# Encoder layer on one core: the down-projection with tokens on partitions in all its columns, and paired one-column products

## The chip, the core and the metric

The kernel runs on one core of a Trainium2 chip. The engines named here are TensorE (PE; its weight loads are listed as PEld), VectorE (DVE), ScalarE (ACT) and the queue of SyncE (SP) that issues most transfers. The metric is the time of one execution on the device in microseconds (us); several runs give a median. The profile is that of one execution, with starts counted from its first instruction.

## The reference

One encoder layer over 256 tokens of width 2048, in float32. What matters here is its end:

```python
x = x + concatenate([y_a, y_b, y_c]) @ w_out[i]        # 2048 x 2048
h = rmsnorm(x, norm_ffn[i])
up = dwconv3(h @ ffn_w_up[i], ...)                     # 2048 -> 2 x 5632
gate, val = jnp.split(up, 2, axis=-1)
x = x + (jax.nn.silu(gate) * val) @ ffn_w_down[i]      # 5632 -> 2048
return rmsnorm(x, norm_final)
```

`rmsnorm` divides a token's 2048 values by the root of their mean square and multiplies them by a weight for each channel.

## The kernel before

**Products.** Every weight arrives from memory as a float32 chunk `raw` of 128x1024 (512 KB; four buffers), is rounded by ACT to `hi` and its remainder taken by DVE as `lo = raw - hi` (three buffers each); this is `load_split` (lines 100 to 117: the cast is L115, the subtraction L116). Activations are kept as such pairs too (`actA`, `actB`, `yT`, `gT`), so that a product takes three terms: hi by hi, lo by hi and hi by lo.

**Channels on partitions.** In the input, output and up-projections, and in most of the down-projection, a weight block of 128x128 stands still in PE and the activations move (`chunk_products`, L144 to L152): for each block of 128 input channels one product with 512 columns (L151: the activation's hi and lo parts of 256 tokens side by side) and one with 256 columns (L152: the weight's lo part by the activation's hi part). Below, such a pair is called one step. `proj_tile` makes one tile of 128 output channels so: 16 steps in the up-projection, 44 in the down-projection. ACT then copies the second half of the sums (L159), and DVE adds the two.

**The down-projection.** Output tiles 0 to 11 (`MD` = 12 of 16) are made that way, by 12 x 44 = 528 steps; to each DVE adds the residual `xT`, ACT squares it (L647) and DVE adds the squares into `acc3`. The last 512 channels have the tokens on partitions: the activation `gT` stands still (128 tokens, hi or lo) and 512 columns of weights move. `products` (L775 to L783) gives three products of 512 columns for each half `h` of the tokens and each block `k`. There the residual enters the sums by eight products with the identity (L759). The first four chunks of those weights are loaded early into `kept`; the half `h = 0` uses them first, and `h = 1` at the very end. `sum_cols(acc3)` (L176, two one-column products) gives the squares of the first 12 tiles. `finish(h)` (L729 to L753) squares the 512 columns, makes the factor of each token, spreads it over partitions by a product (L746), scales everything and sends it out in five transfers for each half: one with tokens on partitions, four with channels on partitions.

**Order.** The tile framework sets the order on each engine from the program order, priorities (a load has an offset of `AHEAD` = 150) and buffers. Each engine executes its own queue in order. `settle` (L132) puts one product of one moving column into the PE's stream and pins its place; it is called twice at the start of the output projection (L659, L660) and once in the up-projection after tile 2 (L693). The one-column product is in float32 and shows as two records, and so does every other product of plain float32 that is not a transposition.

## Time and profile before

| | us |
|---|---|
| median of 3 runs (1071.21 to 1071.91) | 1071.64 |
| the profiled execution | 1071.91 |
| its span, first to last instruction | 1070.0 |
| PE busy | 1059.6 |
| DVE busy | 788.9 |
| ACT busy | 578.6 |

The profiled execution is 1.9 us longer than its span, and it is the longest of the three, 0.27 us above the median. PE is busy nearly all the time. Its products overlap in the records (each row's duration is longer than the distance to the next start), so the distance between starts tells what a product costs in the stream.

### The profile page before, as it was taken

How to read it: one execution, taken by the hardware profiler on the slowest of the kernel's cores; microseconds unless marked ns; L12 is line 12 of the kernel's file. 1: busy time of each engine (PE TensorE's matmuls, PEld its weight loads, DVE VectorE, ACT ScalarE, POOL GpSimd, SP SyncE). 2: the span in 40 equal slices, each digit the busy share in tenths (PEclk: the TensorE clock that was granted, in tenths of full speed). 3: DMA queues.
4: the chain of work that ended last, by engine and by line, in shares of the span. 5: the costliest groups of instructions: out<-in, count | busy, mean ns of one | idle time of the engine just before them, and what ended most of it. 6: DMA issues, size and time to landing. Idle time of an engine off the chain costs nothing.

```text
span 1070.0 us, 15760 instructions
## 1 busy us (share of the span) xinstructions
PE 1059.6 (99%) x5974; PEld 923.6 (86%) x5974; DVE 788.9 (74%) x1241; ACT 578.6 (54%) x876; POOL 1.3 (0%) x14
## 2 busy tenths in 40 slices
PE   9999999999999999999999999999999999999997
PEld 9888898888888888888888888888888888888885
DVE  7899998987768778787777777787876454565344
ACT  7766555555556555555555555555555444454332
POOL 0000000000000000000000000000000000000000
PEclk9999999999999999999999999999999999999999
DMA  8776555655666555655566555655565655666452
GB/s 290 244 229 210 161 164 171 232 172 185 196 194 182 186 186 188 182 192 181 193 181 192 181 192 182 190 184 185 189 188 178 190 183 182 225 214 199 142 191 78
DMA packets 61875, 202.83 MB, mean 190 GB/s; under 512 B 6919, under 2 KB 11752, under 8 KB 61672
## 3 DMA queue, kind: packets, MB, share of 16 engines
q1 hardware_dynamic: 61512, 201.45, 59.2%
q8 instruction: 46, 0.75, 0.3%
q10 hardware_dynamic: 288, 0.39, 0.1%
q14 instruction: 29, 0.24, 0.1%
HBM read 199.72 MB, written 2.10 MB: 189 GB/s over the span
## 4 chain that ended last, share of the span: by engine, by line
PE 96%; DVE 1%; DMA 1%; ACT 1%; issue 0%; SPq 0%; DVEq 0%; ACTq 0%
PE mm L151 57%; PE mm L152 29%; PE mm L781 2%; PE mm L783 2%; PE mm L782 2%; PE mm L264 1%; PE mm L263 1%; PE mm L265 1%; DVE lo L116 1%; DMA head<-in_w_v 1%; PE aux L141 0%; PE aux L142 0%; DMA raw<-in_w_in 0%; PE aux L489 0%; PE aux L140 0%
## 5 line engine op out<-in xcount | busy, mean ns | idle before, releaser
L115 ACT CAST hi<-raw 128x1024 fp32r<-128x1024 f32 (+1 forms) x362 | 373.4, 1031 | 443.7 <-PE mm L151 222.8
L116 DVE TENSOR_TENSOR lo<-raw,hi 128x1024 fp32r<-128x1024 f32 (+1 forms) x362 | 434.6, 1201 | 239.6 <-ACT hi L115 239.0
L151 PE MATMUL mm<-actB,hi 128*128 128x512 f32 x1408 | 497.9, 399 | 0.0
L152 PE MATMUL mm<-actB,lo 128*128 128x256 f32 x1408 | 395.3, 281 | 0.0
L151 PEld LDWEIGHTS mm<-actB,hi 128*128 128x128 f32 x1408 | 264.5, 188 | 66.0 <-DVE actB L668 0.3
L152 PEld LDWEIGHTS mm<-actB,lo 128*128 128x128 f32 x1408 | 265.9, 189 | 0.0
L151 PE MATMUL mm<-gT,hi 128*128 128x512 f32 x528 | 186.6, 399 | 0.0
L152 PE MATMUL mm<-gT,lo 128*128 128x256 f32 x528 | 148.3, 281 | 0.0
L151 PE MATMUL mm<-actA,hi 128*128 128x512 f32 x416 | 148.0, 398 | 0.0
L151 PEld LDWEIGHTS mm<-gT,hi 128*128 128x128 f32 x528 | 99.2, 188 | 24.8
L152 PE MATMUL mm<-actA,lo 128*128 128x256 f32 x416 | 116.2, 279 | 0.0
L152 PEld LDWEIGHTS mm<-gT,lo 128*128 128x128 f32 x528 | 99.7, 189 | 0.0
L151 PEld LDWEIGHTS mm<-actA,hi 128*128 128x128 f32 x416 | 78.1, 188 | 16.9
L151 PE MATMUL mm<-yT,hi 128*128 128x512 f32 x256 | 89.3, 395 | 0.0
L152 PEld LDWEIGHTS mm<-actA,lo 128*128 128x128 f32 x416 | 78.5, 189 | 0.1
L152 PE MATMUL mm<-yT,lo 128*128 128x256 f32 x256 | 71.0, 278 | 0.0
L408 ACT ACTIVATE o<-ev,par 128x256 f32<-128x256 f32 x106 | 63.4, 598 | 7.2 <-DVE ev L403 5.7
L151 PEld LDWEIGHTS mm<-yT,hi 128*128 128x128 f32 x256 | 48.0, 188 | 11.1
L410 DVE SCALAR_TENSOR_TENSOR o<-ev,par,o 128x255 f32<-128x255 f32 x106 | 51.2, 483 | 3.3
L159 ACT COPY sb<-mm 128x256 f32<-128x256 f32 x142 | 51.8, 365 | 0.0
L409 DVE SCALAR_TENSOR_TENSOR o<-ev,par,o 128x255 f32<-128x255 f32 x106 | 50.7, 478 | 0.4 <-ACT o L408 0.4
L152 PEld LDWEIGHTS mm<-yT,lo 128*128 128x128 f32 x256 | 48.1, 188 | 0.0
(226 smaller groups left out, 819.2 us busy)
## 6 DMA issues: line engine op xcount, KB each, us to landing
raw<-in_w_up SPq DMA_DIRECT2D x176, 512.0 KB, 3.5
raw<-in_w_down SPq DMA_DIRECT2D x60, 512.0 KB, 3.6
raw<-in_w_in SPq DMA_DIRECT2D x56, 512.0 KB, 3.6
raw<-in_w_out SPq DMA_DIRECT2D x32, 512.0 KB, 3.5
raw<-in_w_last SPq DMA_DIRECT2D x22, 512.0 KB, 3.5
raw<-in_w_v SPq DMA_DIRECT2D x8, 384.0 KB, 4.4
raw<-in_w_down SPq DMA_DIRECT2D x12, 256.0 KB, 2.6
head<-in_w_v SPq DMA_DIRECT2D x7, 384.0 KB, 6.2
```

The costliest lines, as they stand in the source:

```text
L115: nc.scalar.copy(hi[:, s], raw[:, s])
L116: nc.vector.tensor_sub(lo[:, s], raw[:, s], hi[:, s].bitcast(F32))
L151: nc.tensor.matmul(ps, hi[:, s], act[:, k, :, :], start=k == 0, stop=False)
L152: nc.tensor.matmul(ps[:, :L], lo[:, s], act[:, k, 0, :], start=False, stop=k == nk - 1)
L159: nc.scalar.copy(sb, ps[:, L:])
L263: nc.tensor.matmul(o, actA[:, k, 0, t], hi[:, s], start=k == 0, stop=False)
L408: nc.scalar.activation(o, s, AF.Identity, bias=col(b), scale=col(w1))
L409: nc.vector.scalar_tensor_tensor(o[:, 1:], s[:, :L - 1], col(w0), o[:, 1:], op0=ALU.mult, op1=ALU.add)
L410: nc.vector.scalar_tensor_tensor(o[:, :L - 1], s[:, 1:], col(w2), o[:, :L - 1], op0=ALU.mult, op1=ALU.add)
L781: nc.tensor.matmul(acc[h], lh, hi[:, s], start=False, stop=False)
L782: nc.tensor.matmul(acc[h], lh, lo[:, s], start=False, stop=False)
L783: nc.tensor.matmul(acc[h], ll, hi[:, s], start=False, stop=False)
```

## The change

All 2048 output channels of the down-projection now have the tokens on partitions, as four groups of 512 channels (`NG` = 4). For each group, `group(g)` puts the residual into two accumulators (one for each half of the tokens) by eight transpositions on PE (`is_transpose=True`, where there were eight products with the identity for the last group alone). Then 22 chunks follow, each with `products` for both halves. At a group's end `squares_tok` (ACT, its output in a `raw` buffer) sums the squares of 512 columns, and `weigh` (DVE) multiplies by the final norm's weight `gtok` into the place of `xT`; `gtok` is now 128x2048. The last group still begins and ends with the kept chunks. `finish` has no product any more; it scales four pieces of 128x512 and sends each out. `acc3`, its one-column sums, the products of `finish` and the split of the last chunk into halves of 256 columns are gone.

`settle` now makes two one-column products at a time; the second call in the output projection is removed. Two pads in the memory of the core are 64 bytes smaller.

```diff
@@ -34,7 +34,6 @@
-MD = KT - NL // P
@@ -130,7 +129,9 @@
     def settle():
-        tc.keep_in_program_order(nc.tensor.matmul(aux()[:, 0:1], ones, ones[:, 0:1], start=True, stop=True))
+        pc = aux()
+        for h in range(2):
+            tc.keep_in_program_order(nc.tensor.matmul(pc[:, h:h + 1], ones, ones[:, 0:1], start=True, stop=True))
     def split(hi, lo, src):
         nc.scalar.copy(hi, src)
@@ -242,7 +243,7 @@
     def v_product(then):
         pv = [[psm.tile([P, 512], F32, tag="mm", name="mm") for _ in range(2)] for _ in range(2)]
-        p1.tile([P, 56], F32, name="pad_y")
+        p1.tile([P, 40], F32, name="pad_y")
         head = p1.tile([P, KT // 2, D_GM], F32, tag="yT", name="head")
         for k in range(KT):
             if k == 0:
@@ -657,7 +658,6 @@
             chunk_products(head[m], w_out(m), yT, c, KT)
             if c == m == 0:
                 settle()
-    settle()
     for m in range(KT):
         ps, sb = (head[m], second_half(head[m])) if m < 2 else proj_tile(w_out(m), yT, KT)
         x = xT[:, m, :]
@@ -672,7 +672,7 @@
     p2 = ctx.enter_context(tc.tile_pool(name="p2", bufs=1))
-    p2.tile([P, 64], F32, name="pad_g")
+    p2.tile([P, 48], F32, name="pad_g")
     gT = p2.tile([P, NFF, 2, L], F32R, name="gT")
     rbc2 = p2.tile([P, L], F32, name="rbc_ffn")
@@ -701,98 +701,96 @@
         split(gT[:, j, 0, :], gT[:, j, 1, :], sg)
-    acc3 = p2.tile([P, L], F32, name="acc3")
-    gtok = p2.tile([P, NL], F32, name="gtok")
+    gtok = p2.tile([P, D], F32, name="gtok")
     nc.sync.dma_start(gtok, a["gfin"].partition_broadcast(P))
     NKC = CW // NL
     NC = NFF // NKC
+    NG = D // NL
     NKEEP = KT * L // CW
     kept = big.tile([P, NKEEP, 2, CW], F32R, tag="actA", name="kept")
-    chunks = {}
-    for m in range(MD):
-        c = m - (MD - 1 - NKEEP)
-        if 0 <= c < NKEEP:
-            chunks[c] = load_split(a["w_last"][c], CW, into=(kept[:, c, 0, :], kept[:, c, 1, :]))
-        ps, sb = proj_tile(lambda c, n: a["w_down"][m, c][:, :n], gT, NFF)
-        x = xT[:, m, :]
-        nc.vector.tensor_add(sb, x, sb)
-        nc.vector.tensor_add(x, ps[:, :L], sb)
-        sumsq(acc3, x, m)
-        nc.scalar.activation(x, x, AF.Copy, scale=col(C_GFIN + m))
+    ssq = p2.tile([P, 2, NG], F32, name="ssq")
     rest = p2.tile([P, 2], F32, name="rest")
     c15 = p2.tile([P, 1], F32, name="c15")
     nc.vector.memset(c15, 1.5)
-    def finish(h, ps):
...
-    def products(h, c):
-        hi, lo = chunks[c]
+    res = xT.rearrange("p (g k) l -> p g (k l)", g=NG)
+    def group(g):
+        acc = [bank() for _ in range(2)]
+        for h in range(2):
+            for i in range(NL // P):
+                nc.tensor.matmul(acc[h][:, i * P:(i + 1) * P], xT[:, g * NL // P + i, h * P:(h + 1) * P], ident,
+                                 is_transpose=True, start=i == 0, stop=False)
+        return acc
+    def products(acc, h, w, c, last):
+        hi, lo = w
         for i in range(NKC):
             k = NKC * c + i
             s = slice(i * NL, (i + 1) * NL)
             lh, ll = (gT[:, k, j, h * P:(h + 1) * P] for j in range(2))
             nc.tensor.matmul(acc[h], lh, hi[:, s], start=False, stop=False)
             nc.tensor.matmul(acc[h], lh, lo[:, s], start=False, stop=False)
-            nc.tensor.matmul(acc[h], ll, hi[:, s], start=False, stop=False)
+            nc.tensor.matmul(acc[h], ll, hi[:, s], start=False, stop=last and i == NKC - 1)
+    def squares_tok(g, h, ps):
+        sq = wp.tile([P, CW], F32, tag="raw", name="raw", bufs=4)
+        nc.scalar.activation(sq[:, :NL], ps, AF.Square, accum_out=ssq[:, h, g:g + 1])
+    def out(g, h):
+        return res[:, g, h * NL:(h + 1) * NL]
+    def weigh(g, h, ps):
+        nc.vector.tensor_mul(out(g, h), ps, gtok[:, g * NL:(g + 1) * NL])
+    chunks = {}
+    for g in range(NG - 1):
+        acc = group(g)
+        for c in range(NC):
+            if g == NG - 2 and c % 4 == 3 and c // 4 < NKEEP:
+                j = c // 4
+                chunks[j] = load_split(a["w_down"][NG - 1, j], CW, into=(kept[:, j, 0, :], kept[:, j, 1, :]))
+            w = load_split(a["w_down"][g, c], CW)
+            for h in range(2):
+                products(acc, h, w, c, c == NC - 1)
+        for h in range(2):
+            squares_tok(g, h, acc[h])
+            weigh(g, h, acc[h])
+    nc.vector.tensor_add(rest, ssq[:, :, 0], ssq[:, :, 1])
+    nc.vector.tensor_add(rest, rest, ssq[:, :, 2])
+    nc.vector.tensor_scalar(rest, rest, 1.0 / D, EPS_RMS, op0=ALU.mult, op1=ALU.add)
+    def finish(h, ps):
+        g = NG - 1
+        squares_tok(g, h, ps)
+        weigh(g, h, ps)
+        v, s_, y, w, r = (tmp(f"fin{i}", 1) for i in range(5))
+        nc.scalar.activation(s_, ssq[:, h, g:], AF.Sqrt, scale=1.0 / D, bias=rest[:, h:h + 1])
+        nc.vector.tensor_scalar(v, ssq[:, h, g:], 1.0 / D, rest[:, h:h + 1], op0=ALU.mult, op1=ALU.add)
+        nc.vector.reciprocal(y, s_)
+        nc.vector.scalar_tensor_tensor(w, y, -0.5, y, op0=ALU.mult, op1=ALU.mult)
+        nc.vector.scalar_tensor_tensor(w, w, v, c15, op0=ALU.mult, op1=ALU.add)
+        nc.vector.tensor_mul(r, w, y)
+        for g in range(NG):
+            o = out(g, h)
+            if g == 1:
+                nc.scalar.activation(o, o, AF.Copy, scale=r)
+            else:
+                nc.vector.tensor_scalar(o, o, r, None, op0=ALU.mult)
+            (nc.scalar if g == 1 else nc.sync).dma_start(a["out"][h, :, g * NL:(g + 1) * NL], o)
+    acc = group(NG - 1)
     for c in range(NC):
         if c >= NKEEP:
-            chunks[c] = load_split(a["w_last"][c], CW)
-        (last_products if c == NC - 1 else products)(0, c)
+            chunks[c] = load_split(a["w_down"][NG - 1, c], CW)
+        products(acc, 0, chunks[c], c, c == NC - 1)
         if c >= NKEEP:
-            products(1, c)
-        if c == NKEEP:
-            pc = sum_cols(acc3)
-            nc.vector.tensor_scalar(rest, pc[:, 0:2], 1.0 / D, EPS_RMS, op0=ALU.mult, op1=ALU.add)
+            products(acc, 1, chunks[c], c, False)
     for c in range(NKEEP):
-        (last_products if c == NKEEP - 1 else products)(1, c)
+        products(acc, 1, chunks[c], c, c == NKEEP - 1)
         if c == 1:
             finish(0, acc[0])
     finish(1, acc[1])
```

**PE in the output and up-projections.** `L133` before is `L134` after, the one-column products of `settle`; around it stand the pairs of a step. Before, in three places:

```order
L151 MATMUL mm<-yT,hi 128x512
L152 MATMUL mm<-yT,lo 128x256
L133 MATMUL aux<-ones 128x1
L151 MATMUL mm<-yT,hi 128x512
...
L152 MATMUL mm<-actB,lo 128x256
L176 MATMUL aux<-ones,acc_2522 128x1 x2
L151 MATMUL mm<-actB,hi 128x512
...
L152 MATMUL mm<-actB,lo 128x256
L133 MATMUL aux<-ones 128x1
L151 MATMUL mm<-actB,hi 128x512
```

The first of these places comes twice, 24 steps apart. After the change, the one place in the output projection and the one in the up-projection:

```order
L152 MATMUL mm<-yT,hi 128x512
L153 MATMUL mm<-yT,lo 128x256
L134 MATMUL aux<-ones 128x1 x2
L152 MATMUL mm<-yT,hi 128x512
...
L153 MATMUL mm<-actB,lo 128x256
L134 MATMUL aux<-ones 128x1 x2
L152 MATMUL mm<-actB,hi 128x512
```

The second one-column product of the pair stands directly behind the first; the place 24 steps on holds none.

**PE at the end of group 1, after the change.** `mm_8810` is group 1's accumulator of the second half, `mm_9652` and `mm_9653` are group 3's, `mm_9221` and `mm_9222` group 2's (whose transpositions were already made at the end of group 0); L735 is the last term of a block, L723 a transposition, L733 and L734 the first two terms; names in brackets are what an instruction waits for:

```order
L735 MATMUL mm_8810<-hi_9198,gT_3393 128x512
L723 MATMUL mm_9652<-ident_80,xT_2519 128x128 [waits DVE_49,PE_49]
L723 MATMUL mm_9652<-ident_80,xT_2519 128x128 x3
L723 MATMUL mm_9653<-ident_80,xT_2519 128x128 [waits DVE_49,PE_49]
L723 MATMUL mm_9653<-ident_80,xT_2519 128x128 x3
L733 MATMUL mm_9221<-hi_9232,gT_3393 128x512 [waits Activation_49]
L733 MATMUL mm_9222<-hi_9232,gT_3393 128x512
L734 MATMUL mm_9221<-lo_9233,gT_3393 128x512 [waits DVE_49]
L735 MATMUL mm_9221<-hi_9232,gT_3393 128x512
```

The transpositions stand ahead of the next group's products. At the end of group 0 stand eight of group 1 and then eight of group 2 (16 in a row); at the end of group 2 none.

**ACT and DVE at the same place, after the change.** ACT (L739 is the square of `squares_tok`, L114 the cast of a chunk; `hi_9198` is the last chunk of group 1, `hi_9232` the first of group 2):

```order
L114 CAST hi_9198<-raw_9197 128x1024 [waits DMAHW2_49,DVE_49,PE_49]
L739 ACTIVATE raw_9215,ssq_8393<-mm_8809 128x512 [waits PE_49]
L739 ACTIVATE raw_9218,ssq_8393<-mm_8810 128x512 [waits DVE_49,PE_49]
L114 CAST hi_9232<-raw_9231 128x1024 [waits DMAHW3_49]
L114 CAST hi_9250<-raw_9249 128x1024 [waits DMAHW4_49,DVE_49]
```

DVE (L745 is `weigh`, L115 the subtraction that makes `lo`):

```order
L115 TENSOR_TENSOR lo_9199<-raw_9197,hi_9198 128x1024 [waits DMAHW2_49,Activation_49]
L745 TENSOR_TENSOR xT_2519<-mm_8809,gtok_8390 128x512 [waits Activation_49]
L745 TENSOR_TENSOR xT_2519<-mm_8810,gtok_8390 128x512 [waits Activation_49]
L760 TENSOR_TENSOR rest_8394<-ssq_8393 128x2
L115 TENSOR_TENSOR lo_9233<-raw_9231,hi_9232 128x1024 [waits DVE_49,DMAHW3_49,PE_49,Activation_49]
```

Before, ACT had at the end of a tile of the down-projection casts of the following chunks ahead of the copy of the finished sums (`mm_9871`, L159; `hi_9983` is the tile's last chunk, the three rows behind it are later ones):

```order
L115 CAST hi_9983<-raw_9982 128x512 [waits DMAHW2_49,PE_49]
L115 CAST hi_10042<-raw_10041 128x1024 [waits DMAHW3_49,DVE_49,PE_49]
L115 CAST hi_10064<-raw_10063 128x1024 [waits DMAHW4_49,DVE_49,PE_49]
L115 CAST hi_10082<-raw_10081 128x1024 [waits DMAHW5_49,DVE_49,PE_49]
L159 COPY sb_9996<-mm_9871 128x256 [waits PE_49]
```

What moved: the reading of the finished sums, which stood behind casts of later chunks, stands ahead of all casts of the next group.

## Rows read from the trace of the kernel before

**Rows 1.** The page: the chain that ended last, shares of the span by engine.

```profile
PE 96%; DVE 1%; DMA 1%; ACT 1%; issue 0%; SPq 0%; DVEq 0%; ACTq 0%
```

**Rows 2.** L151 by window: length, PE busy (x), PEld busy (x), granted clock, DMA share, GB/s.

```profile
240.00:318.00 78.00, 78.00 (x226) 42.19 (x225) 1.00 0.63 193
340.00:790.00 450.00, 450.00 (x1275) 239.38 (x1274) 1.00 0.59 186
815.00:995.00 180.00, 180.00 (x511) 95.72 (x510) 1.00 0.63 198
```

**Rows 3.** Timeline of PE, last group: start, duration, engine, line.

```profile
1019.89 0.39 PE L783 MATMUL mm<-hi,gT 128*128 128x512 f32 x1
...
1021.25 0.39 PE L783 MATMUL mm<-hi,gT 128*128 128x512 f32 x1
```

**Rows 4.** Timeline of PE around the four one-column places, with two L151 between places.

```profile
227.10 0.28 PE L133 MATMUL aux<-ones 128*128 128x1 f32 x2
...
227.67 0.40 PE L151 MATMUL mm<-yT,hi 128*128 128x512 f32 x1
...
235.46 0.40 PE L151 MATMUL mm<-yT,hi 128*128 128x512 f32 x1
235.81 0.28 PE L133 MATMUL aux<-ones 128*128 128x1 f32 x2
...
319.81 0.50 PE L176 MATMUL aux<-ones,acc 128*128 128x1 f32 x4
320.17 0.48 PE L151 MATMUL mm<-actB,hi 128*128 128x512 f32 x1
320.60 0.40 PE L151 MATMUL mm<-actB,hi 128*128 128x512 f32 x1
...
325.11 0.39 PE L151 MATMUL mm<-actB,hi 128*128 128x512 f32 x1
331.44 0.28 PE L133 MATMUL aux<-ones 128*128 128x1 f32 x2
```

**Rows 5.** Timeline of PE: products with the identity, those behind them; two transpositions.

```profile
998.75 1.95 PE L759 MATMUL mm<-ident,xT 128*128 128x128 f32 x16
1000.45 0.48 PE L781 MATMUL mm<-kept,gT 128*128 128x512 f32 x1
1000.77 0.39 PE L782 MATMUL mm<-kept,gT 128*128 128x512 f32 x1
...
1001.69 0.40 PE L783 MATMUL mm<-kept,gT 128*128 128x512 f32 x1
...
93.16 0.50 PE L438 MATMUL aux<-ident,z 128*128 128x128 f32 x2
93.42 0.47 PE L151 MATMUL mm<-actA,hi 128*128 128x512 f32 x1
```

**Rows 6.** Groups by line and shape: count | busy us, mean ns | idle before, releaser.

```profile
L116 DVE TENSOR_TENSOR lo<-raw,hi 128x1024 fp32r<-128x1024 f32 x342 | 418.8, 1225 | 229.0 <-ACT hi L115 228.6
...
L115 ACT CAST hi<-raw 128x1024 fp32r<-128x1024 f32 x342 | 359.3, 1050 | 421.9 <-PE mm L151 207.1 <-issue 160.8 <-PE mm L783 29.8
```

**Rows 7.** Timeline of the end: last product, squares, DVE's scaling, first transfer out.

```profile
1061.23 0.28 PE L773 MATMUL mm<-kept,gT 128*128 128x256 f32 x1
1061.55 0.38 ACT L734 ACTIVATE raw<-mm 128x256 f32<-128x256 f32 x1 [4.72 <-PE mm L773]
1061.83 0.19 ACT L734 ACTIVATION_READ_ACCUMULATOR raw<-mm 128x1 f32 x1
1061.92 0.38 ACT L736 ACTIVATE raw<-mm 128x256 f32<-128x256 f32 x1
1063.92 0.75 DVE L747 SCALAR_TENSOR_TENSOR raw<-mm,fin,gtok 128x512 f32<-128x512 f32 x1
1064.70 0.34 SPq L748 DMA_DIRECT2D out_tok<-raw  x1
```

**Rows 8.** All engines by window at the end: the granted clock is the column after POOL.

```profile
1066.40:1066.80 0.40, 0.00 (x0) 0.00 (x0) 0.12 (x1) 0.00 (x0) 0.00 (x0) 0.61 1.05 314
```

More of the change, by code (lines that the diff above doesn't have):

```diff
@@ L727, in encoder_layer @@
     nc.vector.memset(c15, 1.5)
-    def finish(h, ps):
-        t = slice(h * P, (h + 1) * P)
-        wide = wp.tile([P, CW], F32, tag="raw", name="raw", bufs=4)
-        sq, xt = wide[:, :NL], wide[:, NL:]
-        ssq, v, s_, y, w, r, sa, more = (tmp(f"fin{i}", 1) for i in range(8))
-        nc.scalar.activation(sq[:, :L], ps[:, :L], AF.Square, accum_out=sa)
-        nc.vector.tensor_scalar(more, sa, 1.0 / D, rest[:, h:h + 1], op0=ALU.mult, op1=ALU.add)
-        nc.scalar.activation(sq[:, L:], ps[:, L:], AF.Square, accum_out=ssq)
-        nc.scalar.activation(s_, ssq, AF.Sqrt, scale=1.0 / D, bias=more)
-        nc.vector.tensor_scalar(v, ssq, 1.0 / D, more, op0=ALU.mult, op1=ALU.add)
-        nc.vector.reciprocal(y, s_)
-        nc.vector.scalar_tensor_tensor(w, y, -0.5, y, op0=ALU.mult, op1=ALU.mult)
-        nc.vector.scalar_tensor_tensor(w, w, v, c15, op0=ALU.mult, op1=ALU.add)
-        dg = tmp("rms_dg", L, 1)
-        nc.vector.tensor_scalar(dg[:, :P], ident, w, y, op0=ALU.mult, op1=ALU.mult)
-        nc.vector.tensor_mul(r, w, y)
-        pb = aux()
-        nc.tensor.matmul(pb[:, :P], ones, dg[:, :P], start=True, stop=True)
-        nc.vector.scalar_tensor_tensor(xt, ps, r, gtok, op0=ALU.mult, op1=ALU.mult)
-        nc.sync.dma_start(a["out_tok"][h], xt)
-        cuts = [0, 2, 5, 8, MD]
-        for ms in map(slice, cuts, cuts[1:]):
-            xs = xT[:, ms, t]
-            nc.vector.tensor_mul(xs, xs, pb[:, :P].unsqueeze(1).broadcast_to([P, xs.shape[1], P]))
-            nc.sync.dma_start(a["out_ch"][h, :, ms, :], xs)
@@ L755, in encoder_layer @@
-    acc = []
-    for h in range(2):
-        acc.append(psm.tile([P, 512], F32, tag="mm", name="mm"))
-        for i in range(NL // P):
-            nc.tensor.matmul(acc[h][:, i * P:(i + 1) * P], xT[:, MD + i, h * P:(h + 1) * P], ident, start=i == 0,
-                             stop=False)
-    def last_products(h, c):
-        hi, lo = chunks[c]
-        for g in range(2):
-            o = acc[h][:, g * L:(g + 1) * L]
-            for i in range(NKC):
-                k = NKC * c + i
-                s = slice(i * NL + g * L, i * NL + (g + 1) * L)
-                lh, ll = (gT[:, k, j, h * P:(h + 1) * P] for j in range(2))
-                nc.tensor.matmul(o, lh, hi[:, s], start=False, stop=False)
-                nc.tensor.matmul(o, lh, lo[:, s], start=False, stop=False)
-                nc.tensor.matmul(o, ll, hi[:, s], start=False, stop=g == 1 and i == NKC - 1)
@@ L775, in products @@
-    def products(h, c):
-        hi, lo = chunks[c]
+    res = xT.rearrange("p (g k) l -> p g (k l)", g=NG)
[8 more added lines that the diff above has]
+        hi, lo = w
@@ L898 @@
     down = i["ffn_w_down"][0]
-    last = down[:, MD * P:].reshape(-1, CW // NL, P, NL).transpose(0, 2, 1, 3).reshape(-1, P, CW)
+    down = down.reshape(-1, CW // NL, P, D // NL, NL).transpose(3, 0, 2, 1, 4).reshape(D // NL, -1, P, CW)
     arrays = {
@@ L917 @@
         "w_up": _tiles(up),
-        "w_down": _tiles(down[:, :MD * P]),
-        "w_last": last,
-        "gfin": i["norm_final"][MD * P:],
+        "w_down": down,
+        "gfin": i["norm_final"],
         **_constants(),
@@ L927 @@
          for k, v in arrays.items()}
-    a["out_ch"] = nc.dram_tensor("out_ch", (2, P, MD, P), F32, kind="ExternalOutput").ap()
-    a["out_tok"] = nc.dram_tensor("out_tok", (2, P, NL), F32, kind="ExternalOutput").ap()
+    a["out"] = nc.dram_tensor("out", (2, P, D), F32, kind="ExternalOutput").ap()
     with tile.TileContext(nc) as tc:
@@ L932 @@
     r = run(nc, [{f"in_{k}": v for k, v in arrays.items()}], core_ids=[0])
-    ch, tok = r.results[0]["out_ch"], r.results[0]["out_tok"]
-    ch = ch.transpose(0, 3, 2, 1).reshape(L, MD * P)
-    return np.ascontiguousarray(np.concatenate([ch, tok.reshape(L, -1)], axis=1)[None])
+    return np.ascontiguousarray(r.results[0]["out"].reshape(1, L, D))
```

## The prediction

> **What bounds the kernel now.** I read the page first. The chain of work that ended last is PE's for 96% of the span [rows 1], so a change counts by what it does to the stream of products, or by making PE wait. Since the records of products overlap, I then took distances between starts. Windows of L151 give the length of a step (one product of 512 columns, one of 256) as length over count: 78 us hold 225 steps, 0.3467 us each, in the output projection; 450 us hold 1274, 0.3532 us, in the up-projection; 180 us hold 510, 0.3529 us, in the down-projection [rows 2]. The same instructions run at two step lengths, 6.6 ns apart, while the granted clock is 1.00 (2.4 GHz) in all three rows.
>
> The timeline shows where the length changes [rows 4]. After the first single one-column product (227.10) steps are long: 7.79 us for 22, 0.354. After the second (235.81) they are short, and they still are behind the pair of `sum_cols` (319.81): 13 steps from 320.60 to 325.11 take 0.347 us each. Behind the single product at 331.44 they are long, through the whole up-projection and, with no interruption that changes it, the down-projection. An interruption can move PE from one length to the other; without one it keeps its length.
>
> Products of 512 columns alone, the form with tokens on partitions, follow each other every 0.2267 us: six in 1.36 us [rows 3].
>
> **The products of the down-projection.** Removed: 528 steps at 0.353 = 186.4 us. Added: three groups x 22 chunks x 12 = 792 products at 0.2267 = 179.5 us. That is 6.9 us less. Weights, casts and subtractions stay in number and size: per chunk ACT needs 1.05 and DVE 1.23 us [rows 6] against 2.72 us of PE (12 x 0.2267), so they stay covered inside a group.
>
> The Trainium skill, "TensorE: Matmul & The Clock Gate", section "Back-to-back issue gap", speaks against this gain: columns at 2.4 GHz plus 2.5 ns, 0.216 us for 512 columns and 0.109 for 256. By it a step would take 0.325 us and the gain would be 171.6 - 170.9 = 0.7 us. The rows differ (0.353 and 0.2267), and the measurement decides.
>
> **The residual.** Removed: eight products with the identity, 1.70 us, and 0.09 us in the distance behind them (0.32 where 0.23 is usual) [rows 5]: 1.8 us. Added: 32 transpositions. A pair of them takes 0.26 us until the next product starts, 0.13 each [rows 5]; long runs are not in the trace. Bounds for one: 0.106 (a record of the identity products, 1.70/16) and 0.22 (if only the last is cheap). Group 0's eight cost 1.1 us with re-entry (0.9 to 1.9); the other 24 fall into the waits that follow.
>
> **The new wait at a group's end.** ACT's queue now has both squares of a finished group ahead of the next group's casts, and DVE's has both `weigh` ahead of the next subtractions; both wait for PE's last product. So no chunk of the next group is ready when PE arrives. Let S be the start of that last product. It ends at S+0.39 [rows 3]; ACT's square starts 0.04 us after such an end [rows 7], at S+0.43. A square of 256 columns takes 0.38, a cast of 1024 1.05 [rows 6, 7], so one of 512 about 0.60; by the same rows the next ACT instruction starts some 0.58 later, S+1.0, and the sum is read out at S+1.1. The first cast runs from there to S+2.05. DVE's second `weigh` (0.75 us for 512 columns at L747 [rows 7]; I take 0.7) ends at S+1.85, its first subtraction runs from S+2.1 to S+3.3, and PE's first `lo` product starts at S+3.35. Ahead of it PE has done its last product and two `hi` products (0.68 us) and the transpositions, whose last four wait for `weigh` until S+1.9. Lost: 2.7 us at the ends of groups 0 and 1, **5.4 us**. The end of group 2 costs nothing, because the last group starts with 24 products on kept chunks (5.4 us), which cover those 3.3 us. At its start group 0 has its casts ahead, as a tile had. The `raw` buffers of the third and fourth chunk also wait for the squares, at S+1.1 at the latest; PE wants them from S+8.3 on, and I take seven microseconds as cover enough for transfer, cast and subtraction (what comes later than S+8.3 would be lost). Lower bound for the two ends: the 24 transpositions alone at 0.11, 2.7 us. Upper bound: a further cast and subtraction ahead at each, 10.0 us.
>
> **Small terms.** The sums of `acc3` and two products of `finish` go: the pair of one-column products takes 0.36 us [rows 4] and about 0.09 for re-entry; one product of `finish` lies inside the stream and I give it 0.25. Together -0.7. One-column products in `settle` grow from three to four: +0.2. The split halves of the last chunk: nothing. The end: the first transfer is issued 3.47 us after the last product's start [rows 7] and the rest takes 5.3 us. After: square and sum 1.1, `weigh` to 1.85, then five short operations and the first scaling, for which I take 1.6 together, so the same moment; then the same 1 MB, without the product and with fewer pieces on DVE. I take -0.4 (-1.0 to +0.7). The larger `gtok` (1 MB for 256 KB) goes out early in the up-projection, where weights land ahead of a cast that waits for PE; nothing, and up to 3 us if that cover were gone.
>
> These sum to -6.9 - 1.8 + 1.1 + 5.4 - 0.7 + 0.2 - 0.4 = **-3.1 us**.
>
> **The step length after the pairs.** This is the largest term. Up-projection: 85 tiles x 16 = 1360 steps follow the pair after tile 2. If they are short, 1360 x 6.6 ns = 9.0 us are gained; if long, nothing. Four interruptions by one-column products are in the trace. Of the three singles one left short steps, and the one that met short steps made them long; the one pair (319.81) met short ones and left them short [rows 4]. The new place has the pair's form, so short is likelier. In the output projection the pair stands where the first single left long steps; if short, 24 steps gain 0.2 us, if long, 240 steps lose 1.6 us until the pair of `sum_cols`. I take short for both: -9.2.
>
> Against this profile's own 1071.9 us: 1071.9 - 3.1 - 9.2 = 1059.6. The profiled run lies 0.27 us above the median, so I predict **1059.5 us**. A difference under 0.2% (2.1 us: 1069.5 to 1073.8) can hardly be told from none here.
>
> **Rivals.**
> *Long steps in the up-projection.* One record of a pair is thin evidence, and a single did turn short to long. Then 1071.6 - 3.1 - 0.2 = 1068.3; with long steps in the output projection too, 1070.1. The group form alone hardly pays, since its two waits take back most of its gain.
>
> *The clock falls at the group ends.* It fell within 1066.4 to 1066.8 [rows 8], 5 us after the last dense product (1061.23) [rows 7]. A group's end has 3.1 us with only transpositions and two products, shorter than that; but if it fell at both and stayed at half for as long as the fall took, 5 us, each would cost 2.5 us: 1064.5.
> The Trainium skill, same page, "PE-mode transpose", says that transpositions do not count as PE activity, which would make this likelier. No run here shows it.
>
> *Slower: the longer distance in all new products.* The first products after the identity run were 0.92 us for four, 0.231 each, until they fell to 0.2267 [rows 3, 5]. If tokens-on-partitions products kept 0.2333, the same 6.6 ns more, all 1056 would cost 7.0 us on top of 1068.3 and of 1.6 in the output projection: 1076.9. It decides once the distance exceeds about 0.230. Against it: they fell within seven products and stayed.
>
> **How the numbers follow.** Forecast 0.58 (own range 1057.5 to 1062); long steps in the up-projection 0.29, of which 0.10 with the output projection long; clock 0.08; slower 0.05. Faster: 0.58 + 0.08 + most of 0.19 = 0.83; same 0.12; slower 0.05. Low end: the forecast with the waits at their lower bound, 1057. High end: 1070, which takes in the first rival and leaves out under 2 in 10.
>
> **What the profile after would show.** Windows over the up-projection with 0.3467 us for each step (one in 0.353 refutes the main term); 0.680 us for three products inside a group; at the ends of groups 0 and 1 an idle PE until a subtraction on DVE, with casts on ACT idle until PE, some 3.3 us from the last product to the first `lo` product, and none at group 2's; transpositions near 0.13 us; clock 1.00. The prediction is wrong if the steps stay long, if the ends of groups cost more than 5 us each, or if the output projection loses its short steps.

## The result, and the profile after

The changed kernel takes 1060.40 us (median of four runs, 1059.09 to 1061.48) where the kernel before takes 1071.46: a ratio of 0.9896, 95% interval 0.9879 to 0.9913. It is faster by 1%, and the time lies 0.9 us from the forecast. The profiled run took 1060.88 us, with a span of 1059.1.

The page's chain that ended last is still PE's, as before [rows 1]; ACT has a little more of it:

```profile
PE 96%; ACT 2%; DVE 1%; DMA 1%; issue 0%; DVEq 0%; SPq 0%; ACTq 0%
```

The windows of [rows 2] for the line of the 512-column products, now L152 (length, PE busy with the count, PEld busy, granted clock, DMA share, GB/s):

```profile
240.00:318.00 78.00, 78.00 (x222) 41.52 (x221) 1.00 0.59 189
340.00:790.00 450.00, 450.00 (x1299) 242.75 (x1299) 1.00 0.58 190
```

The two lengths have changed places. In the up-projection 450 us hold 1298 steps (one less than the count, as in the prediction), 0.3467 us each, where they held 1274; in the output projection 78 us hold 221, 0.353 each, where they held 225. The granted clock is 1.00 in both.

The timeline of PE where the stages begin, at the transpositions of group 0, and at the last product:

```profile
224.52 0.45 PE L152 MATMUL mm<-yT,hi 128*128 128x512 f32 x1
...
315.46 0.40 PE L152 MATMUL mm<-actB,hi 128*128 128x512 f32 x1
...
805.30 1.03 PE L723 MATMUL mm<-ident,xT 128*128 128x128 f32 x8
806.09 0.47 PE L733 MATMUL mm<-hi,gT 128*128 128x512 f32 x1
806.40 0.39 PE L734 MATMUL mm<-lo,gT 128*128 128x512 f32 x1
...
1050.99 0.39 PE L735 MATMUL mm<-kept,gT 128*128 128x512 f32 x1
```

In the trace before the same boundaries lie at 224.23, 313.69, 812.19 and 1061.23 us (the last in [rows 7]). The differences give the time by stage:

| us | before | after | difference | forecast |
|---|---|---|---|---|
| up to the output projection | 224.23 | 224.52 | +0.29 | 0 |
| output projection | 89.46 | 90.94 | +1.48 | -0.2 |
| up-projection | 498.50 | 489.84 | -8.66 | -9.0 + 0.2 |
| down-projection | 249.04 | 245.69 | -3.35 | -2.9 |
| from the last product's start to the end | 8.74 | 8.08 | -0.66 | -0.4 |
| span | 1069.97 | 1059.07 | -10.90 | -12.3 |

The end of group 0, PE first, then ACT and DVE in the same stretch (what ended an idle time stands in brackets):

```profile
865.81 0.39 PE L735 MATMUL mm<-hi,gT 128*128 128x512 f32 x1
866.05 1.47 PE L723 MATMUL mm<-ident,xT 128*128 128x128 f32 x12
867.80 0.63 PE L723 MATMUL mm<-ident,xT 128*128 128x128 f32 x4 [0.28 <-DVE xT L745]
868.19 0.71 PE L733 MATMUL mm<-hi,gT 128*128 128x512 f32 x2
869.18 0.51 PE L734 MATMUL mm<-lo,gT 128*128 128x512 f32 x1 [0.28 <-DVE lo L115]
```

```profile
866.24 0.60 ACT L739 ACTIVATE raw<-mm 128x512 f32<-128x512 f32 x1 [0.67 <-PE mm L735]
866.74 0.19 ACT L739 ACTIVATION_READ_ACCUMULATOR raw<-mm 128x1 f32 x1
866.83 1.98 ACT L114 CAST hi<-raw 128x1024 fp32r<-128x1024 f32 x2
...
866.97 0.69 DVE L745 TENSOR_TENSOR xT<-mm,gtok 128x512 f32<-128x512 f32 x1 [0.67 <-ACT raw L739]
867.90 2.36 DVE L115 TENSOR_TENSOR lo<-raw,hi 128x1024 fp32r<-128x1024 f32 x2 [0.24 <-ACT hi L114]
```

Read it from the bottom up. PE's first `lo` product (869.18) waits for DVE's subtraction (867.90), that for the cast (866.83), that for the second square (866.24), and that for PE's last product (865.81): 3.37 us, of which 0.68 are products. At the end of group 1 the same chain runs from 928.48 to 931.84; at the end of group 2 PE has no gap. What PE shows as idle (twice 0.28 us) is only a part of the loss: sixteen transpositions, 0.109 us from start to start, fill 1.7 us of it, and records overlap. The distance between starts shows the whole. The granted clock through both waits (all engines by window; it is the column after POOL's count):

```profile
864.00:872.00 8.00, 7.43 (x40) 5.92 (x39) 4.96 (x5) 4.52 (x8) 0.00 (x0) 1.00 0.56 167
926.50:935.00 8.50, 7.25 (x35) 5.35 (x34) 5.04 (x6) 4.89 (x8) 0.00 (x0) 1.00 0.59 176
```

At the end of the kernel the granted clock falls (PE alone; the clock is the column after PE's count):

```profile
1054.40:1054.80 0.40, 0.00 (x0) 0.72 0.00 0
1054.80:1055.20 0.40, 0.00 (x0) 0.50 0.35 123
```

The end, which answers to [rows 7] (the square, the factor of the token, the scaling, the transfers):

```profile
1051.42 0.60 ACT L739 ACTIVATE raw<-mm 128x512 f32<-128x512 f32 x1 [2.91 <-PE mm L735]
1052.14 0.69 DVE L745 TENSOR_TENSOR xT<-mm,gtok 128x512 f32<-128x512 f32 x1 [3.07 <-ACT raw L739]
...
1053.70 1.28 DVE L782 TENSOR_SCALAR xT<-xT,fin 128x512 f32<-128x512 f32 x3
1054.21 1.31 SPq L783 DMA_DIRECT2D out<-xT  x3
```

The first transfer goes out 3.22 us after the last product's start (3.47 before).

### The profile page after: what moved, and what is told of

The parts are those of the page before. It is cut to its first block, busy times and chain, and to the rows that moved or that the text cites. A ratio compares the mean times of both kernels' runs of the same rounds, so it can differ in the third digit from the quotient of the medians.

```text
span 1059.1 us, 15128 instructions
## 1 busy us (share of the span) xinstructions
PE 1047.2 (99%) x5708; PEld 910.5 (86%) x5708; DVE 776.1 (73%) x1202; ACT 569.7 (54%) x844; POOL 1.3 (0%) x14
## 4 chain that ended last, share of the span: by engine, by line
PE 96%; ACT 2%; DVE 1%; DMA 1%; issue 0%; DVEq 0%; SPq 0%; ACTq 0%
PE mm L152 44%; PE mm L153 23%; PE mm L734 8%; PE mm L735 8%; PE mm L733 7%; PE mm L264 1%; PE mm L265 1%; PE mm L266 1%; ACT hi L114 1%; DVE lo L115 1%; DMA raw<-in_w_in 1%; PE aux L142 0%; PE aux L96 0%; PE aux L490 0%; PE aux L143 0%
## 5 line engine op out<-in xcount | busy, mean ns | idle before, releaser
L115 DVE TENSOR_TENSOR lo<-raw,hi 128x1024 fp32r<-128x1024 f32 (+1 forms) x356 | 433.3, 1218 | 225.0 <-ACT hi L114 224.6
L114 ACT CAST hi<-raw 128x1024 fp32r<-128x1024 f32 (+1 forms) x356 | 372.5, 1047 | 419.4 <-issue 171.8
L152 PE MATMUL mm<-actB,hi 128*128 128x512 f32 x1408 | 489.0, 392 | 0.0
L153 PE MATMUL mm<-actB,lo 128*128 128x256 f32 x1408 | 394.3, 280 | 0.0
L152 PEld LDWEIGHTS mm<-actB,hi 128*128 128x128 f32 x1408 | 263.3, 187 | 58.0 <-DVE actB L668 0.2
L153 PEld LDWEIGHTS mm<-actB,lo 128*128 128x128 f32 x1408 | 266.1, 189 | 0.0
L152 PE MATMUL mm<-actA,hi 128*128 128x512 f32 x416 | 148.0, 398 | 0.0
L734 PE MATMUL mm<-lo,gT 128*128 128x512 f32 x336 | 130.9, 390 | 0.6 <-DVE lo L115 0.6
L735 PE MATMUL mm<-hi,gT 128*128 128x512 f32 x336 | 130.7, 389 | 0.0
L733 PE MATMUL mm<-hi,gT 128*128 128x512 f32 x336 | 130.5, 390 | 0.0
L153 PE MATMUL mm<-actA,lo 128*128 128x256 f32 x416 | 116.1, 279 | 0.0
L152 PEld LDWEIGHTS mm<-actA,hi 128*128 128x128 f32 x416 | 78.1, 188 | 16.9
L152 PE MATMUL mm<-yT,hi 128*128 128x512 f32 x256 | 90.7, 399 | 0.0
L153 PEld LDWEIGHTS mm<-actA,lo 128*128 128x128 f32 x416 | 78.4, 188 | 0.1
L734 PEld LDWEIGHTS mm<-lo,gT 128*128 128x128 f32 x336 | 63.1, 188 | 14.6 <-DVE lo L115 1.4
L735 PEld LDWEIGHTS mm<-hi,gT 128*128 128x128 f32 x336 | 63.1, 188 | 12.9
L733 PEld LDWEIGHTS mm<-hi,gT 128*128 128x128 f32 x336 | 62.9, 188 | 12.9
L153 PE MATMUL mm<-yT,lo 128*128 128x256 f32 x256 | 71.9, 281 | 0.0
L152 PEld LDWEIGHTS mm<-yT,hi 128*128 128x128 f32 x256 | 48.1, 188 | 11.9
```

Source lines behind the costliest of these rows:

```text
L114: nc.scalar.copy(hi[:, s], raw[:, s])
L115: nc.vector.tensor_sub(lo[:, s], raw[:, s], hi[:, s].bitcast(F32))
L152: nc.tensor.matmul(ps, hi[:, s], act[:, k, :, :], start=k == 0, stop=False)
L153: nc.tensor.matmul(ps[:, :L], lo[:, s], act[:, k, 0, :], start=False, stop=k == nk - 1)
L733: nc.tensor.matmul(acc[h], lh, hi[:, s], start=False, stop=False)
L734: nc.tensor.matmul(acc[h], lh, lo[:, s], start=False, stop=False)
```

## The experiments

My theory was that the step length is set where the stream is interrupted and that the group ends cost 2.7 us each; the main rival, that something else in the change made the steps short. First the two halves of the change ran alone; then the interruption and the waits at the group ends were taken away.

**The settle edit alone** on the kernel before (`settle_alone`):

```diff
-        tc.keep_in_program_order(nc.tensor.matmul(aux()[:, 0:1], ones, ones[:, 0:1], start=True, stop=True))
+        pc = aux()
+        for h in range(2):
+            tc.keep_in_program_order(nc.tensor.matmul(pc[:, h:h + 1], ones, ones[:, 0:1], start=True, stop=True))
...
             if c == m == 0:
                 settle()
-    settle()
```

> The kernel before, with the edit of settle alone: one pair of one-column products in the output projection and one pair after tile 2 of the up-projection, in place of three single ones. My theory: the step length is set where the stream is interrupted, and a pair keeps the length that it meets. Then the up-projection's 1360 steps take 0.3467 us (-9.0 us), and the 528 steps of the down-projection, which follow without an interruption that changes it, inherit that (528 x 6.6 ns = -3.5 us); the output projection loses its short steps as in the changed kernel (+1.6 us). Sum: 1071.5 - 9.0 - 3.5 + 1.6 = 1060.6 us, no slower than the whole change. Rival: the length comes from what else the change moves (addresses, the order of loads around the larger gtok), and the steps stay at 0.3533: 1071.5 to 1073.

Measured: 1059.18 us (1058.69 to 1059.66, four runs), ratio 0.9877 (0.9863 to 0.9892). Its windows of L153, up-projection and down-projection:

```profile
340.00:790.00 450.00, 450.00 (x1299) 243.38 (x1298) 1.00 0.61 190
815.00:985.00 170.00, 170.00 (x491) 91.97 (x491) 1.00 0.65 202
```

Both have steps of 0.347 us. The down-projection of before, left as it was, now takes 245.50 us (802.68 to 1048.18) where the new one takes 245.69. Here the pair in the output projection left short steps (225 steps in 78 us), so the 1.6 us of the expectation did not come. The settle edit alone is worth as much as the whole change.

**The down-projection alone**, with the three single products of before (`down_alone`, the reverse of that edit on the changed kernel):

> The changed kernel with the three single one-column products of before. My theory: the single one after tile 2 makes the steps of the up-projection 0.3533 us again (+9.0 us), the second single one in the output projection gives short steps there (-1.6 us): 1060.4 + 9.0 - 1.6 = 1067.8 us, some 3.5 us faster than before. Rival, by which something else in the change made the steps short: 1060 us or less.

Measured: ten runs in two groups, five from 1060.11 to 1060.93 us and five from 1068.35 to 1070.01. The window of L150 in the up-projection of the profiled run, which took 1068.35:

```profile
340.00:790.00 450.00, 450.00 (x1275) 239.28 (x1274) 1.00 0.59 186
```

In the profiled execution the steps are long, as expected; the five faster times speak against it for every execution. And the second single product in the output projection left long steps there, not short ones. So a single product does not simply lengthen.

**No interruption after tile 2**, on the kernel before (`before_no_up`):

```diff
-            if m == 2:
-                settle()
```

> The kernel before without the single one-column product after tile 2 of the up-projection; nothing else. My theory: the steps are short (0.347 us) from the second settle of the output projection on, and only that single product makes them long, so the up-projection and the down-projection keep 0.347: 1071.5 - 9.0 - 3.5 - 0.2 = 1058.8 us. Rival: long steps are what PE falls back to when no settle holds it, and the time stays at 1071.4.

Measured: 1059.25 us (1058.03 to 1059.67), ratio 0.9876 (0.9861 to 0.9891), with 1298 steps in 340 to 790 us. Taking one one-column product out of the old kernel brings what the whole change brings.

**Squares out of the ring of raw buffers** (`sq_own`):

```diff
-        sq = wp.tile([P, CW], F32, tag="raw", name="raw", bufs=4)
-        nc.scalar.activation(sq[:, :NL], ps, AF.Square, accum_out=ssq[:, h, g:g + 1])
+        nc.scalar.activation(out(g, h), ps, AF.Square, accum_out=ssq[:, h, g:g + 1])
```

> The changed kernel, in which the squares of squares_tok go to the place of xT that weigh overwrites afterwards, and no longer into a raw buffer. My theory: the squares took their turn in the ring of raw buffers, so that the next group's loads and casts could not be put ahead of them; now two casts and subtractions of the next group stand ahead of the first square, and PE goes on without a wait at the ends of groups 0 and 1. The two waits of 2.69 us go (-5.4 us), and the eight transpositions at the starts of groups 1, 2 and 3, which lay in the waits, count again (3 x (8 x 0.109 + 0.1) = +2.9 us): 1060.4 - 2.5 = 1057.9 us. Rival: PE waits for something else that is late at the same place (the third cast, or weigh that now stands behind subtractions), and the time stays at 1060.

Measured: 1056.78 us (1055.81 to 1059.17), ratio 0.9858 (0.9840 to 0.9875). The end of group 0 in its trace, PE and then ACT:

```profile
865.16 0.39 PE L735 MATMUL mm<-hi,gT 128*128 128x512 f32 x1
865.39 1.03 PE L723 MATMUL mm<-ident,xT 128*128 128x128 f32 x8
866.18 0.48 PE L733 MATMUL mm<-hi,gT 128*128 128x512 f32 x1
866.49 0.39 PE L734 MATMUL mm<-lo,gT 128*128 128x512 f32 x1
```

```profile
862.86 1.06 ACT L114 CAST hi<-raw 128x1024 fp32r<-128x1024 f32 x1 [1.66 <-PE mm L735]
864.22 0.60 ACT L738 ACTIVATE xT<-mm 128x512 f32<-128x512 f32 x1 [0.30 <-PE mm L735]
```

One cast of the next group (862.86; two were expected) comes ahead of the squares, the first `lo` product follows 1.33 us after the last product, and the down-projection takes 242.76 us (804.62 to 1047.38), 2.93 less (2.5 expected). The wait came from where the square's unused output was put.

**Products with the identity** in place of transpositions, in `sq_own` (`sq_identity`):

```diff
-                                 is_transpose=True, start=i == 0, stop=False)
+                                 start=i == 0, stop=False)
```

> As sq_own, with the residual put into the sums by products with the identity (as the kernel before did for its last group) instead of transpositions. By the trace of sq_own eight transpositions and the re-entry behind them cost 0.88 us at each of the four starts of groups; by the trace of before eight identity products cost 1.70 + 0.09 us. So +0.9 us at each of four starts: 1056.8 + 3.6 = 1060.4 us. Rival: the transposition only moves work that PE would have hidden, and the time stays at 1057.

Measured: 1060.25 us (1059.33 to 1061.45). Its down-projection takes 246.33 us (803.16 to 1049.49), 3.57 more. Where nothing hides them, eight transpositions cost 0.9 us and eight identity products 1.8.

**The change again** (`after_again`, the same kernel once more):

> The changed kernel once more, beside the others on one chip. Theory: its up-projection is short in every run, since the pair keeps short steps, and what varies between runs is the output projection (short or long, 1.6 us) and the start: 1058.5 to 1061.5, by its profile with short steps in the output projection 1.6 us less than with long ones. Rival: as with the single products of down_alone, some runs are 9 us slower.

Measured: 1060.61 us (1058.88 to 1060.98), ratio 0.9892 (0.9878 to 0.9907), short steps in the up-projection. Its trace too has 222 products of 512 columns in the 78 us of the output projection (long), so the short case that I expected to see is not among its records.

**Many interruptions in one trace.** `many_single` and `many_pair` call settle after every tile from tile 2 on, the first with a single product:

```diff
-            if m == 2:
+            if m >= 2:
                 settle()
```

> The changed kernel with single one-column products, and in the up-projection one of them after every tile from tile 2 on: 86 places in one trace. A place costs 0.22 us (at 331.4 of the trace before: 0.257 us from the last product of a step to the next step where 0.117 is usual, and 0.314 behind it where 0.235 is usual), together +18.5 us: 1078.9 us if all steps are short. Theory A, a single product always swaps the two lengths: short and long tiles in turn, 4.5 us more, 1083.4. Theory B, after the runs so far: a single that meets short steps makes them long (three of three in the traces), one that meets long steps makes them short about every second time: about two thirds of the tiles long, 1085. Theory C, the length does not hang on the interruptions: one length throughout, 1078.9 or 1087.9.

> The changed kernel with its pair of one-column products after every tile of the up-projection from tile 2 on: 86 places in one trace. A pair costs 0.45 us: 85 more of them +38 us, 1098.6 us with short steps. Theory B, after the runs so far: a pair keeps short steps short (seven of seven in the traces) and turns long ones short about every second time, so after a few tiles at the latest every tile is short. Theory A', a pair leaves either length at random: half of the tiles long, +4.5 us, 1103.

Measured: 1083.49 and 1099.01 us, one run each. PE's rows in `many_single` at five places in a row:

```profile
331.19 0.28 PE L132 MATMUL aux<-ones 128*128 128x1 f32 x2
...
337.06 0.28 PE L132 MATMUL aux<-ones 128*128 128x1 f32 x2
...
342.94 0.28 PE L132 MATMUL aux<-ones 128*128 128x1 f32 x2
...
348.71 0.28 PE L132 MATMUL aux<-ones 128*128 128x1 f32 x2
...
354.59 0.28 PE L132 MATMUL aux<-ones 128*128 128x1 f32 x2
```

The distances are 5.87, 5.88, 5.77 and 5.88 us, that is 16 steps of 0.3533 or 0.3467 and 0.22 for the product: long, long, short, long. That order holds to the last tile, without an exception. None of the three theories had it: not a swap, not chance, not one length. The time alone would have passed for theory A (1083.4) by luck: the trace has more long tiles than A, and an output projection 1.9 us shorter than the changed kernel's. In `many_pair` every tile behind the first of the 86 pairs is short, as expected.

**Another distance** (`single_24`: single products 24 steps apart, in the middle of tile 4, after tile 5 and so on), and **a wide product in turn with the single one** (`single_wide`: behind odd tiles a float32 product of 256 columns, `settle_wide`, which stands in the last diff below):

```diff
-        return proj_tile(lambda c, n: a["w_up"][m, c][:, :n], actB, KT)
+        between = settle if m >= 3 and m % 3 == 1 else None
+        return proj_tile(lambda c, n: a["w_up"][m, c][:, :n], actB, KT, between=between)
...
-            if m == 2:
+            if m >= 2 and m % 3 == 2:
                 settle()
```

```diff
-            if m == 2:
-                settle()
+            if m >= 2:
+                settle() if m % 2 == 0 else settle_wide(rbc2)
```

> As many_single, but with 24 steps between the single one-column products in place of 16 (57 places). In many_single the tiles went short, long, long, short, long, long without an exception. Theory D, a counter: a single product moves PE on by one of three positions, one of which is short, whatever lies between; then the stretches go short, long, long again: 1059.8 + 57 x 0.22 + 2/3 x 9 = 1078.4 us. Theory E, a phase: the steps themselves go round with a period of three (16 steps leave a remainder of one, 24 none), so that with 24 steps another order comes out: short and long in turn, as at the two places of the output projection 24 steps apart (1076.9), or one length throughout (1072.4 short, 1081.4 long).

> As many_single, but behind every second tile (odd ones) stands a float32 product of 256 columns in place of the one-column product. In the traces so far the one such product (the spreading of the factors, ahead of tile 2) left short steps whether it met short or long ones. Theory: that holds in general. Then all 43 tiles behind a wide product are short, and the tiles behind a single one are long (a single that met short steps made them long in every place so far): 1059.8 + 43 x 0.22 + 43 x 0.43 + 4.5 = 1092.3 us. Rival: the wide product only keeps the length, as a pair does, and three places were chance: the tiles behind it are as those ahead, and the order short, long, long of the singles shows with doubled length.

Measured, one run each: 1076.36 us, in the order long, long, short again: theory D. It is 2.0 us under D's sum; 1.9 of them are the output projection, which was short. And 1087.14 us: behind every wide product the steps are short, but after the first tile a single product that meets them leaves them short as well, so the expected 4.5 us did not come.

The starts of the records in nanoseconds show what decides; the timeline's two decimals do not. Call the two products of a step `hi` (512 columns) and `lo` (256 columns). Short steps come in two forms, with 232 ns on average from the `hi` to the `lo` product and 115 on to the next step, or 230 and 117. Long steps go round with a period of three: about 241, 236 and 232 ns from `hi` to `lo`. The table sorts all places in the output and up-projections of the 14 traces (before, after and the last run below included) by what stood ahead, and gives what came behind; "last distance" is that from `hi` to `lo` in the last step ahead:

| interruption | met short 232/115 | met short 230/117 | met long, last distance 236 | met long, last 241 or 232 |
|---|---|---|---|---|
| one column, single | long, 53 of 53 | short, 43 of 43 | short, 54 of 54 | long, 49 of 49 |
| one column, pair | short, 12 of 12 | short, 87 of 87 | long, 3 of 3 | short, 3 of 3 |
| 256 columns, float32 | short, 50 of 50 | short, 1 of 1 | short, 1 of 1 | short, 5 of 5 |

Five pairs are not in it, those of `sum_cols` that met long steps, where PE had waited a step ahead of them: four left long steps, one short. Of the 12 pairs in the first column nine are of `sum_cols` too, with such a wait. Most places lie in four traces, and the cells of one to five places are thin.

**The two groups of `down_alone`**, with the same kernel once more:

> down_alone once more, since its ten executions fell into two groups (five at 1060.1 to 1060.9 us, five at 1068.4 to 1070.0) and the trace so far shows one of the slower group. There are two forms of short steps in the traces: 0.232 + 0.115 us and 0.230 + 0.117. A single one-column product that met the first form always left long steps, one that met the second form always left short ones (42 places of single_wide). Theory: the group is decided at the single product after tile 2 by the form ahead of it. An execution near 1060 us then shows steps of 0.230 + 0.117 ahead of that place and short steps behind it, one near 1069 us steps of 0.232 + 0.115 ahead and long ones behind. Rival: the same form ahead of the place with either outcome, that is, chance at the place itself; or the slower group loses its 9 us elsewhere.

Measured: 1060.43 us. Ahead of its single product after tile 2 the starts are 230 and 117 ns apart, and the steps behind it are short (the row below, of L150); in the trace of the 1068.35 us run they were 232 and 115. The theory holds for both. The two traces part at `sum_cols`: both met long steps there, and its pair left short ones of 230 and 117 in the slower execution and long ones in the faster. The wide product that spreads the factors turned these into 232 and 115, and into 230 and 117.

```profile
340.00:790.00 450.00, 450.00 (x1300) 243.40 (x1299) 1.00 0.61 190
```

**A better version** (`wide_out`): `sq_own`, a wide product in the output projection, none after tile 2.

```diff
+    def settle_wide(src):
+        tc.keep_in_program_order(nc.tensor.matmul(aux()[:, :L], ones, src, start=True, stop=True))
...
-                settle()
+                settle_wide(xT[:, 0, :])
...
-            if m == 2:
-                settle()
```

> sq_own with a float32 product of 256 columns as the interruption in the output projection, and none after tile 2 of the up-projection. My theory: the wide product always leaves short steps, in the output projection as well, where the pair left long ones in two of the five traces with a pair there (1.6 us each); and the up-projection is short from the wide product ahead of tile 2 on, so that the pair after it is only cost (0.45 us). The wide product costs 0.43 us, as the pair does. Against sq_own: -0.45 and less spread: 1056.3 us, 1055.5 to 1057.5, no run with long steps in the output projection. Rival: long steps come back somewhere, in the output projection (+1.6) or in the up-projection (+9).

Measured: 1055.33 us (1055.08 to 1056.07, five runs), ratio 0.9847 (0.9834 to 0.9861): the lowest of all, 0.2 us under the range expected, and the spread of its five runs is 1.0 us where the changed kernel's four had 2.4. In the two traces the up-projection gained the 0.45 us expected (489.66 us in `sq_own`, 489.21 here); what came on top lies ahead of the output projection, and why stays open. Steps are short in both projections (windows of L150):

```profile
240.00:318.00 78.00, 78.00 (x226) 42.19 (x226) 1.00 0.61 199
340.00:790.00 450.00, 450.00 (x1299) 243.38 (x1298) 1.00 0.60 190
```

## Why the prediction was right, and where it was not

**Step length in the up-projection: the size right, the way there in part luck.** Short steps gave 8.7 us of the span's 10.9, as forecast. But the one pair on record then had met short steps, and the forecast took the output projection to be short too; that failed. In the kernel after, 13 steps from 322.44 take 0.353 us each and 13 from 328.53 take 0.347: the product that spreads the factors (L195, 256 columns) met long steps and left short ones, and the pair (L134) only did no harm.

```profile
322.44 0.40 PE L152 MATMUL mm<-actB,hi 128*128 128x512 f32 x1
...
327.03 0.40 PE L152 MATMUL mm<-actB,hi 128*128 128x512 f32 x1
327.40 0.59 PE L195 MATMUL aux<-rms_dg,ones 128*128 128x256 f32 x2
...
328.53 0.39 PE L152 MATMUL mm<-actB,hi 128*128 128x512 f32 x1
...
333.03 0.39 PE L152 MATMUL mm<-actB,hi 128*128 128x512 f32 x1
333.38 0.50 PE L134 MATMUL aux<-ones 128*128 128x1 f32 x4
```

The prediction does not count that product among the interruptions. What counted was that the single product after tile 2, which met steps of 232 and 115 in the kernel before, is gone: `before_no_up` takes out that product alone and has the whole gain. The caveat "One record of a pair is thin evidence" was fair; the table now has 99 pairs that met short steps and left them short. The "single did turn short to long" of the main rival is true for one form of short steps and not for the other.

**Step length in the output projection: wrong.** The step that failed is "I take short for both", and the loss of these short steps is one of the signs of being wrong that the prediction names. The pair met long steps whose last distance was 236 ns, the one case of the table in which a pair leaves them long (3 of 3), and the 240 steps until `sum_cols` cost 1.5 us where 0.2 were to be gained. The other side of that choice had been priced (1.6 us), so the miss stays inside the range.

**The products: right.** Between the waits the products follow each other every 0.2267 us: 1055 distances make 239.1 us, and with group 0's start (0.90), the two waits (5.37) and the longer distances just behind each wait (0.30 for both) 245.7, which is the stage. The longer distance of the slower rival, 0.2333, did not come.
The Trainium skill, "TensorE: Matmul & The Clock Gate", section "Back-to-back issue gap", gives 0.216 us for the isolated product of 512 columns and 0.131 us for one in a sustained stream; the trace agrees with neither (0.2267). An estimate of a step by the Trainium skill's formula for isolated products, 0.325 us, is under the rows too (0.3467 or 0.3533).

**The waits: right.** First `lo` product 3.37 and 3.36 us after the last product, 3.35 forecast; 5.37 us lost, 5.4 forecast; none at the end of group 2. `sq_own` shows the cause by taking it away.

**The transpositions: a size off.** 0.109 us each between starts, not 0.13, so group 0's start costs 0.90 us and not 1.1. The waits hid the other 24, as forecast: `sq_own` gained only 2.9 of the waits' 5.4 us, because three groups then pay for their own transpositions.

**The clock: right that it holds.** It was 1.00 through both waits, against the second rival. It fell only at the end, between 1054.4 and 1054.8 us, some 3.5 us after the last product's start. The argument for it was weaker than it looks: the prediction sets the 3.1 us of a group's end against a fall 5 us after the last dense product, and in that trace a product of `finish` stands between, less than 3 us ahead of the fall:

```profile
1063.80 0.49 PE L746 MATMUL aux<-rms_dg,ones 128*128 128x128 f32 x2 [2.29 <-DVE rms_dg L743]
```

The Trainium skill, "TensorE: Matmul & The Clock Gate", section "PE-mode transpose", says that transpositions do not count as PE-busy in the same way. No run here shows it: the waits with sixteen and eight of them had products on both sides and kept the clock (1.00), so they don't contradict it either.

**What the sum hid.** The forecast set the new down-projection against long steps (-6.9 us for the products). Against short ones, 528 x 0.3467 = 183.1 us, the gain is 3.5, and residual, waits and all together leave nothing: 245.69 us against the 245.50 of `settle_alone`, with 0.7 us gained behind the last product. The change is faster because of what it does to the calls of settle. The re-tiled down-projection pays only once its group ends are mended (242.76).

## What to carry to other kernels

When PE bounds a kernel, compare the distance between starts of equal instructions in different stages before anything is re-tiled: 6.6 ns in each of 1,900 steps were 1.2% of this kernel, and deleting one one-column product brought them back. A buffer whose content nobody reads still takes its turn in its ring, and with it the place of the loads behind it; write such output where something is overwritten anyway. A term that is the difference to a state which the same change removes should be counted against both states.

## What the runs showed that I had not expected

The stream of alternating 512- and 256-column products has several stable rhythms at a granted clock of 1.00, two with 0.3467 us for a step and one with 0.3533, and keeps the one it is in for over a thousand steps. An interruption shifts it in the same way at every place of the table: in `many_single` and `single_24` three single one-column products bring it round to where it was, a pair kept short steps in 99 of 99 places, a float32 product of 256 columns left them short in 57 of 57. What in PE makes these rhythms stays open. A wide product that met the form 232/115 left that form in 9 places, all of them the product that spreads the factors, and the other form in 41, all of them calls of `settle_wide` in `single_wide`; why is open too. So is what decides, from one execution to the next, the point of the period at which the output projection's first interruption falls. With the same pair there the stage took 90.94 us in both traces of the changed kernel and 89.3 us in those of `settle_alone`, `sq_own` and `sq_identity`; that this makes the changed kernel's spread is likely but not shown.
